# Loading the last three batches of a mixture of softmaxes head by head, instead of the last two

## Chip, cores and metric

One core of one Trainium2 chip. The metric is device time in microseconds (us), the median of several runs; less is better.

## The reference

32 batches, 128 positions, 4 heads, a vocabulary of 4096, all float32. Each head's logits go through a softmax over the vocabulary, and the four are added with weights that are a softmax of `prior`:

```python
# logits (32, 128, 4, 4096), prior (32, 128, 4)
prior_probs = softmax(prior, axis=-1)
softmax = np.exp(logits - logits.max(-1, keepdims=True)); softmax /= softmax.sum(-1, keepdims=True)
mixture = np.sum(prior_probs[..., None] * softmax, axis=2)      # (32, 128, 4096)
```

268 MB are read and 67 MB written: 8 MB (MiB) in and 2 MB out for each batch.

## The kernel before

Positions lie on the 128 partitions. Three engines matter: ACT (ScalarE) computes the exponentials, DVE (VectorE) scales and adds them, and SP (SyncE) issues the transfers to and from memory. A transfer is shared by 16 DMA engines, which move it in *packets*: here one packet is the contiguous bytes of one partition, 64 KB for four heads and 16 KB for one. A batch is one load tile of 4 heads x 16 KB per partition. Two such tiles are in use in turn, and so are two exponential tiles (`etile`) and two accumulators (`acc`). All loads of logits and all stores are issued by SP into one DMA queue, in program order.

```python
lpool = tile_pool(name="lpool", bufs=2)   # load tiles, 64 KB per partition each
epool = tile_pool(name="epool", bufs=2)   # exponentials of one head, 16 KB
apool = tile_pool(name="apool", bufs=2)   # accumulator of one batch, 16 KB

def pieces(b):
    return 1 if b >= B - 2 else H         # heads per transfer

def load(b):
    lt = lpool.tile([P, H, V], FP32, name="ltile")
    n = pieces(b)
    for h in range(0, H, n):
        nc.sync.dma_start(out=lt[:, h : h + n], in_=logits[b, :, h : h + n, :])
    ltiles[b] = lt

load(0); ...; load(1); ...                # and the softmax of prior: cut
for b in range(B):
    last, inplace = b == B - 1, b >= B - 2
    lt = ltiles.pop(b)
    acc = lt[:, 0] if inplace else apool.tile(...)
    for h in range(H):
        split = last and h == H - 1
        et = lt[:, h] if inplace else epool.tile(...)
        nc.scalar.activation(et, lt[:, h], AF.Exp, accum_out=dsum)         # L98, ACT
        # coeff = prior weight / dsum: two small DVE operations, L101 and L102
        if h == 0:   nc.vector.tensor_scalar_mul(acc, et, coeff)           # L104, DVE
        elif not split: nc.vector.scalar_tensor_tensor(acc, et, coeff, acc, mult, add)  # L106
        else:        ...  # the same in four chunks, two stores of 1 MB: L112
    if b + 2 < B: load(b + 2)             # issue L45; waits until ACT has read the whole tile of b
    if b < B - 4: store(b)                # issue L51
    elif b == B - 3: store(b - 1); store(b)
    elif b == B - 2: store(b)
```

So at the end the queue holds: load 28, store 26, load 29, store 27, load 30, load 31, store 28, store 29, store 30, and store 31 in two halves. Batches 30 and 31, which are loaded head by head, also work in place in their load tile.

The softmax here doesn't subtract the row's maximum and nothing guards it: scores larger than these inputs give would overflow.

## Time and profile before

| | before |
|---|---|
| time, median of 3 runs | 786.17 us (785.93 to 786.95) |
| steady batch (first exponential to first exponential) | 24.18 us, 10.49 MB |
| landing step of an 8 MB load, late in the run | 19.31 us |
| landing step of a 2 MB store | 4.87 us |
| loads 30 and 31, in four transfers each | 19.55 and 19.57 us |

A *landing* is the moment when the last of the 16 DMA engines has reported a transfer complete, as recorded in the trace. A *step* is the time from the landing before it in the queue to this one.

From the page of the kernel before: span; DVE and ACT busy time; GB/s in 40 equal slices; the queue with its share of the 16 engines' span; the chain that ended last; and two groups (busy us, mean ns of one | idle before them, and who ended it).

```profile
span 784.6 us, 1001 instructions
...
DVE 547.3 (70%) x408; ACT 472.6 (60%) x258; POOL 0.2 (0%) x4
...
GB/s 378 428 438 451 428 428 407 452 434 421 428 423 446 457 424 434 417 427 443 428 428 435 426 455 431 435 428 416 446 428 451 431 428 426 449 428 413 428 433 307
...
q1 hardware_dynamic: 10224, 335.55, 99.4%
...
DMA 63%; DVE 16%; ACT 13%; issue 6%; DVEq 0%; ACTq 0%; SPq 0%
...
L98 ACT ACTIVATE etile<-ltile 128x4096 f32<-128x4096 f32 x120 | 433.4, 3612 | 280.8 <-DMA ltile<-in_logits_dram 241.5
...
L104 DVE TENSOR_SCALAR acc<-etile,coeff 128x4096 f32<-128x4096 f32 x30 | 70.6, 2353 | 22.1 <-DMA out_dram<-acc 22.0
...
```

The compute engines are idle 30 and 40% of the time; the one DMA queue is busy for 99.4% of the span. Two stretches of the kernel before (columns: stretch, length, busy time and instructions of DVE, ACT, POOL, TensorE clock, DMA share, GB/s):

```profile
...
core 0: us, DVE busy (x) ACT busy (x) POOL busy (x), PEclk, DMA share, GB/s
300.00:690.00 390.00, 272.07 (x194) 235.59 (x128) 0.00 (x0) 1.00 1.00 433
765.00:785.00 20.00, 10.83 (x10) 2.44 (x2) 0.00 (x0) 1.00 0.72 303
...
```

433 GB/s in the middle lies at the ceiling: the Trainium skill, "DMA: Bandwidth & Descriptors", Specifications, gives 435 GB/s as the fabric limit of one core, and this trace agrees. The last 20 us are far below it (303 GB/s), as the 16 engines run out of work one after another.

The stretch that the change touches, from the timeline of the kernel before (start us, length us, engine, line, operation; in brackets how long the engine was idle before it and who ended that):

```profile
...
693.22 0.34 SPq L51 DMA_DIRECT2D out_dram<-acc  x1
...
711.64 25.92 SPq L45 DMA_DIRECT2D ltile<-in_logits_dram  x8
...
719.76 3.62 ACT L98 ACTIVATE etile<-ltile 128x4096 f32<-128x4096 f32 x1 [8.15 <-DMA ltile<-in_logits_dram]
...
724.63 2.35 DVE L104 TENSOR_SCALAR acc<-etile,coeff 128x4096 f32<-128x4096 f32 x1 [0.77 <-DMA out_dram<-acc]
...
727.08 3.62 ACT L98 ACTIVATE etile<-ltile 128x4096 f32<-128x4096 f32 x1
...
732.07 3.62 ACT L98 ACTIVATE etile<-ltile 128x4096 f32<-128x4096 f32 x1 [1.29 <-DVE rden L101]
...
```

Store 27 is issued at 693.22. At 711.64 begin the issues of loads 30 and 31 (eight, merged into one line). The exponentials of batch 29 start at 719.76, when load 29 has landed. DVE's first long step of batch 29 (the scaling, L104) starts at 724.63: its accumulator was free when store 27, which stands behind load 29 in the queue, had landed. The third and fourth exponentials follow at 727.08 and 732.07, each when DVE has given back an etile.

### The profile page before, as it was taken

What the parts mean: (1) busy time and instruction counts of PE and PEld (TensorE: products, weight loads), DVE (VectorE), ACT (ScalarE), POOL (GpSimd) and SP (SyncE); (2) the same over time, 40 slices, a digit from 0 to 9 for tenths busy, and PEclk for the clock granted to TensorE, in tenths of its full rate; (3) what the DMA queues carried; (4) which work ended last, traced back from release to release, by engine and by line L of the source; (5) the groups of instructions that cost most, each with busy time, mean ns of one, the idle gap of its engine ahead of it and who ended that gap; (6) DMA issues with size and microseconds to landing.
All of it is one profiled execution on the core that took longest, in us unless ns stands there. A gap on an engine that the chain in (4) does not pass through costs nothing.

```text
span 784.6 us, 1001 instructions
## 1 busy us (share of the span) xinstructions
DVE 547.3 (70%) x408; ACT 472.6 (60%) x258; POOL 0.2 (0%) x4
## 2 busy tenths in 40 slices
DVE  3588567866678666786667866668756687666995
ACT  0777554675546755467555676555765557755981
POOL 0000000000000000000000000000000000000000
DMA  9999999999999999999999999999999999999997
GB/s 378 428 438 451 428 428 407 452 434 421 428 423 446 457 424 434 417 427 443 428 428 435 426 455 431 435 428 416 446 428 451 431 428 426 449 428 413 428 433 307
DMA packets 10280, 335.68 MB, mean 428 GB/s; under 512 B 1152, under 2 KB 1152, under 8 KB 1184
## 3 DMA queue, kind: packets, MB, share of 16 engines
q1 hardware_dynamic: 10224, 335.55, 99.4%
q10 hardware_dynamic: 48, 0.07, 0.0%
q14 instruction: 8, 0.07, 0.0%
HBM read 268.50 MB, written 67.11 MB: 428 GB/s over the span
## 4 chain that ended last, share of the span: by engine, by line
DMA 63%; DVE 16%; ACT 13%; issue 6%; DVEq 0%; ACTq 0%; SPq 0%
DMA ltile<-in_logits_dram 59%; ACT etile L98 13%; DVE acc L106 11%; DMA out_dram<-acc 3%; DVE ltile L106 3%; DVE ltile L104 1%; DVE rden L101 1%; DVE coeff L102 1%; DVE ltile L112 0%; DVE acc L104 0%; DVEq L152 0%; ACTq L98 0%; SPq L45 0%; DVEq L104 0%
## 5 line engine op out<-in xcount | busy, mean ns | idle before, releaser
L98 ACT ACTIVATE etile<-ltile 128x4096 f32<-128x4096 f32 x120 | 433.4, 3612 | 280.8 <-DMA ltile<-in_logits_dram 241.5
L106 DVE SCALAR_TENSOR_TENSOR acc<-etile,coeff,acc 128x4096 f32<-128x4096 f32 x90 | 403.6, 4484 | 3.2
L101 DVE RECIPROCAL rden<-dsum 128x1 f32<-128x1 f32 x128 | 20.4, 160 | 186.4 <-ACT etile L98 183.3
L104 DVE TENSOR_SCALAR acc<-etile,coeff 128x4096 f32<-128x4096 f32 x30 | 70.6, 2353 | 22.1 <-DMA out_dram<-acc 22.0
L98 ACT ACTIVATE ltile<-ltile 128x4096 f32<-128x4096 f32 x8 | 28.8, 3606 | 2.5 <-DVE coeff L102 1.2
L102 DVE TENSOR_TENSOR coeff<-rden,pp 128x1 f32<-128x1 f32 x128 | 20.4, 159 | 4.4
L106 DVE SCALAR_TENSOR_TENSOR ltile<-ltile,coeff 128x4096 f32<-128x4096 f32 x5 | 22.4, 4485 | 0.2
L98 ACT ACTIVATION_READ_ACCUMULATOR etile<-ltile 128x1 f32 x120 | 22.4, 186 | 0.0
L60 DVE TENSOR_REDUCE pmax<-pr 32x128 f32<-32x512 f32 x1 | 0.7, 674 | 11.4 <-DMA pr<-in_prior_dram 11.4
L64 ACT ACTIVATE pe<-pc 32x512 f32<-32x512 f32 x1 | 0.6, 628 | 10.4 <-DVE pc L62 10.4
L112 DVE SCALAR_TENSOR_TENSOR ltile<-ltile,coeff 128x1024 f32<-128x1024 f32 x4 | 4.9, 1278 | 0.0
L104 DVE TENSOR_SCALAR ltile<-ltile,coeff 128x4096 f32<-128x4096 f32 x2 | 4.7, 2354 | 0.1
L64 ACT ACT_TABLE_LOAD x1 | 1.3, 1283 | 1.2 <-PEq L141 1.2
L78 DVE STREAM_TRANSPOSE pp<-pn 32x32 f32<-32x32 f32 x16 | 1.9, 170 | 0.1
L98 ACT ACTIVATION_READ_ACCUMULATOR ltile<-ltile 128x1 f32 x8 | 1.5, 186 | 0.0
L66 DVE TENSOR_REDUCE psum<-pe 32x128 f32<-32x512 f32 x1 | 0.7, 675 | 0.7 <-ACT pe L64 0.7
L71 DVE TENSOR_TENSOR pn<-pe,prec 32x512 f32<-32x512 f32 x1 | 1.0, 1020 | 0.0
L68 DVE RECIPROCAL prec<-psum 32x128 f32<-32x128 f32 x1 | 0.9, 942 | 0.0
L62 DVE TENSOR_TENSOR pc<-pr,pmax 32x512 f32<-32x512 f32 x1 | 0.7, 679 | 0.0
L141 POOL MEMSET const-bfloat16-1.0<- 128x1 bf16 x1 | 0.1, 101 | 0.0
L141 POOL MEMSET const-uint8-127<- 128x1 uint8 x1 | 0.1, 101 | 0.0
L141 POOL MEMSET const-float32-0.0<- 128x1 f32 x1 | 0.1, 98 | 0.2 <-issue 0.2
(1 smaller groups left out, 0.1 us busy)
## 6 DMA issues: line engine op xcount, KB each, us to landing
out_dram<-acc SPq DMA_DIRECT2D x30, 2048.0 KB, 31.4
ltile<-in_logits_dram SPq DMA_DIRECT2D x8, 2048.0 KB, 22.2
out_dram<-ltile SPq DMA_DIRECT2D x1, 2048.0 KB, 20.4
out_dram<-ltile SPq DMA_DIRECT2D x2, 1024.0 KB, 7.8
ltile<-in_logits_dram SPq DMA_DIRECT2D x30, 32.3
pr<-in_prior_dram ACTq DMA_DIRECT2D x1, 64.0 KB, 10.7
```

What stands on the lines that cost most here:

```text
L60: nc.vector.reduce_max(pmax, pr, axis=AX.X)
L62: nc.vector.tensor_sub(pc, pr, pmax.unsqueeze(2).to_broadcast([B, S, H]))
L64: nc.scalar.activation(pe, pc, AF.Exp)
L68: nc.vector.reciprocal(prec, psum)
L71: nc.vector.tensor_mul(pn.rearrange("b h s -> b s h"), pe, prec.unsqueeze(2).to_broadcast([B, S, H]))
L78: nc.vector.transpose(pp[32 * t : 32 * (t + 1), h, :], pn[:, h, 32 * t : 32 * (t + 1)])
L98: nc.scalar.activation(et, lt[:, h], AF.Exp, accum_out=dsum)
L101: nc.vector.reciprocal(rden, dsum)
L102: nc.vector.tensor_mul(coeff, rden, pp[:, h, b : b + 1])
L104: nc.vector.tensor_scalar_mul(out=acc, in0=et, scalar1=coeff)
L106: nc.vector.scalar_tensor_tensor(out=acc, in0=et, scalar=coeff, in1=acc, op0=ALU.mult, op1=ALU.add)
L112: nc.vector.scalar_tensor_tensor(out=acc[:, cs], in0=et[:, cs], scalar=coeff, in1=acc[:, cs], op0=ALU.mult, op1=ALU.add,)
```

## The change

Its intent is to let the third last batch, too, start on its first head instead of waiting for all four, to shorten the end of the kernel.

```diff
     def pieces(b):
-        return 1 if b >= B - 2 else H
+        return 1 if b >= B - 3 else H
```

Only batch 29 changes: four transfers of 2 MB with packets of 16 KB, where there was one of 8 MB with packets of 64 KB. Batch 29 keeps its separate accumulator and exponential tiles.

## The prediction

> **What bounds the kernel now.** The DMA queue, end to end. The page gives it 99.4% of the 16 engines' span (335.5 MB, 428 GB/s), against DVE 70% and ACT 60%. A steady batch takes 24.18 us (first exponentials at 647.22 and 671.40 in the timeline) and moves 10.49 MB: 434 GB/s. The Trainium skill, "DMA: Bandwidth & Descriptors", Specifications, has 435 GB/s as the fabric ceiling; the trace agrees. The trace's landings step 19.31 us for an 8 MB load and 4.87 us for a 2 MB store, without a gap, to the end: the last three stores land at 778.98, 781.41 and 783.84 of a span of 784.65.
>
> **What the change does.** Batch 29 is loaded by four 2 MB transfers (16 KB per partition) instead of one of 8 MB (64 KB). Bytes, order in the queue, exponentials and vector work stay. Three DMA issues (0.33 to 0.43 us) are added on an idle sequencer.
>
> *Intended gain:* batch 29's first exponential, which waits 8.2 us for the whole load (timeline, 719.76), may start at about 712.5, when batch 28 frees the buffers: 7 us earlier. It leads nowhere. The vector engine's first step of batch 29 waits for the accumulator, freed by the store of batch 27, which lands at 724.53, behind the whole load of 29. The third exponential waits for an etile buffer from that step, the fourth for the next. So the last exponential of batch 29 still ends at about 735.6, and the load of batch 31, which needs the whole buffer, is issued as late as now. Even if it went out earlier, the queue has 8 us of backlog there.
>
> *Cost:* a 16 KB packet takes 611 ns in the trace, a 64 KB packet 2418, and 4 x 611 = 2444. Loads 30 and 31, in pieces already, step 19.55 and 19.57 us per batch, against 19.31 to 19.33. My estimate is +0.24 us, all on the critical path, because the queue is. The fixed 2 us per DMA (same page, "Anatomy of one DMA") will not show: the pieces of loads 30 and 31 run back to back in this trace.
>
> **Time:** 786.17 + 0.24 = 786.4 us. Range 785.7 to 787.3, from the runs' spread (785.93 to 786.95) and chance: an instruction fetch on the same DMA engines (at 774.7) makes one landing step 5.63 instead of 4.87 us; the change could move such a hit by 0.8 us either way. Faster by over 2%: 0.5%; within 2%: 99%; slower by over 2%: 0.5%.
>
> **What would show each step.** Pieces of load 29 landing near 705.0, 709.9, 714.8 and 719.9. First exponential of batch 29 near 712.5; the ACT-on-load waits fall by about 8 us, from 241.5. The vector engine's wait for the store of batch 27 grows from 0.8 to about 7 us. Third and fourth exponentials of batch 29 at about 727.3 and 732.3, the issue of load 31 at about 735.9, and all later landings, 0.2 to 0.3 later than now. DMA share still 99%.
>
> **What would make it wrong.** If smaller transfers let the slowest of the 16 engines catch up (they land up to 4.9 us apart), the time could fall by tenths of a us or more. If the extra transfers use up completion semaphores and a later issue waits for an old one, a queue gap appears and the time rises by several us. If load 29 and store 27 changed places in the queue, the accumulator's wait would change too.

## The result, and the profile after

| | before | after |
|---|---|---|
| first comparison, median | 786.39 us (4 runs) | 785.82 us (785.24 to 786.54, 4 runs) |
| ratio, 95% interval | | 0.9993, 0.9976 to 1.001 |
| second comparison, median | 785.95 us (9 runs) | 786.36 us (785.70 to 786.97, 5 runs) |
| ratio, 95% interval | | 1.0007, 0.9995 to 1.002 |

Ratios and intervals are taken from the times of the fast runs and not from the medians, so a ratio is not quite that of the medians quoted beside it. The time is the same: once 0.6 us under, once 0.4 us over, while the kernel before alone scatters from 784.72 to 787.11.

The same lines of the page of the changed kernel:

```profile
span 783.5 us, 1004 instructions
...
DVE 547.2 (70%) x408; ACT 472.7 (60%) x258; POOL 0.2 (0%) x4
...
GB/s 385 458 405 415 428 435 417 460 432 435 428 407 449 428 428 432 441 426 458 432 428 421 428 443 428 432 442 417 464 432 432 428 412 445 432 421 432 431 428 343
...
q1 hardware_dynamic: 10656, 335.55, 99.6%
...
DMA 62%; DVE 18%; ACT 12%; issue 6%; DVEq 0%; ACTq 0%; SPq 0%
...
L98 ACT ACTIVATE etile<-ltile 128x4096 f32<-128x4096 f32 x120 | 433.5, 3613 | 279.4 <-DMA ltile<-in_logits_dram 232.4
...
L104 DVE TENSOR_SCALAR acc<-etile,coeff 128x4096 f32<-128x4096 f32 x30 | 70.6, 2353 | 24.9 <-DMA out_dram<-acc 24.9
...
```

And its stretches, with the columns as above:

```profile
...
core 0: us, DVE busy (x) ACT busy (x) POOL busy (x), PEclk, DMA share, GB/s
300.00:690.00 390.00, 273.57 (x196) 235.62 (x128) 0.00 (x0) 1.00 1.00 433
765.00:785.00 20.00, 9.31 (x7) 1.33 (x2) 0.00 (x0) 1.00 0.73 311
...
```

The timeline of the changed kernel at the same place:

```profile
...
691.92 0.34 SPq L51 DMA_DIRECT2D out_dram<-acc  x1
...
710.32 25.62 SPq L45 DMA_DIRECT2D ltile<-in_logits_dram  x8
...
711.37 3.62 ACT L98 ACTIVATE etile<-ltile 128x4096 f32<-128x4096 f32 x1 [1.07 <-issue]
...
719.90 0.16 DVE L101 RECIPROCAL rden<-dsum 128x1 f32<-128x1 f32 x1 [3.56 <-ACT etile L98]
...
723.49 2.35 DVE L104 TENSOR_SCALAR acc<-etile,coeff 128x4096 f32<-128x4096 f32 x1 [3.24 <-DMA out_dram<-acc]
...
725.93 3.62 ACT L98 ACTIVATE etile<-ltile 128x4096 f32<-128x4096 f32 x1 [6.07 <-issue]
...
730.45 3.62 ACT L98 ACTIVATE etile<-ltile 128x4096 f32<-128x4096 f32 x1 [0.81 <-ACT etile L98]
...
```

This profiled run is 1.32 us ahead of the profiled run of before when load 28 lands (694.17 against 695.49), a point up to which both kernels issue the same work. Take that off before comparing. Then:

- The first exponential of batch 29 starts at 711.37 instead of 719.76: the intended gain is there. ("issue" in its brackets means that the profile shows no releaser; it starts 0.1 us after a DVE step of batch 28 has ended and given back an etile. So does the one at 725.93, after DVE's multiplication.)
- It is spent on waiting. DVE idles 3.56 us ahead of the reciprocal at 719.90 and 3.24 us more for store 27, whose landing starts the multiplication at 723.49. The third and fourth exponentials, at 725.93 and 730.45, are as late as before (727.25 and 731.77 with the 1.32 us added).

The sums over the whole run, from the waits of before and then of after (engine and line, what it waited for: us in total, times, longest us):

```profile
...
ACT etile L98 <- DMA ltile<-in_logits_dram: 241.5, 30, 10.1
...
DVE acc L104 <- DMA out_dram<-acc: 22.0, 28, 1.2
...
```

```profile
...
ACT etile L98 <- DMA ltile<-in_logits_dram: 232.4, 29, 10.0
...
DVE acc L104 <- DMA out_dram<-acc: 24.9, 28, 3.2
...
```

ACT's wait for loads falls by 9.1 us, and the longest wait of DVE for a store grows from 1.2 to 3.2 us.

The landings show what the queue paid:

| landing, us | before | after | after, second profile |
|---|---|---|---|
| load 28 | 695.49 | 694.17 | 694.89 |
| store 27 (load 29 is ahead of it) | 724.53 | 723.47 | 724.16 |
| difference | 29.05 | 29.30 | 29.27 |
| last store | 783.84 | 782.48 | 783.47 |
| load 28 to last store | 88.35 | 88.31 | 88.57 |

(Differences are taken before rounding.) From the landing of load 28 to that of store 27, with store 26 and load 29 between them, it takes 0.25 and 0.22 us longer; load 29 alone steps 19.50 and 19.53 us, instead of 19.31. That the whole tail of the first profile is nevertheless not longer seems to have another reason: an instruction fetch on the DMA engines (at 774.7 us before, at 773.4 after) comes just ahead of a long landing step of store 30, 5.63 us in before, 5.34 us in after and 5.61 us in the second profile, instead of 4.87. Take off the excess of each and the tails are 87.59, 87.84 and 87.83 us: +0.25 and +0.24.

And the 1.32 us at the start? In the kernel before, a fetch at 558.7 us is followed by one load step of 20.19 instead of 19.31 us; in the changed kernel a fetch at 559.5 us is followed by a step of 19.30. In these profiles a fetch occupies one engine for 0.31 us, and the packet behind it takes 0.25 to 0.64 us longer than others of its size. At 558.7 us that is 0.31 + 0.60 us, near the 0.88 us by which the step is longer. In the landings it shows only in some of the profiles, as one would expect if it counts only where it meets the engine that is furthest behind (argued, not tested). The rest of the 1.32 us was there at load 16 (404.39 against 403.96), from uneven steps in the first 400 us. So the 1.2 us by which the profile's span is shorter (783.46 against 784.65) arose ahead of the changed load.

### The profile page after: what moved, and what is told of

Read it like the earlier page. It is cut to its first block, busy times and chain, and to the rows that moved or that the text cites. A ratio compares the mean times of both kernels' runs of the same rounds, so it can differ in the third digit from the quotient of the medians.

```text
span 783.5 us, 1004 instructions
## 1 busy us (share of the span) xinstructions
DVE 547.2 (70%) x408; ACT 472.7 (60%) x258; POOL 0.2 (0%) x4
## 4 chain that ended last, share of the span: by engine, by line
DMA 62%; DVE 18%; ACT 12%; issue 6%; DVEq 0%; ACTq 0%; SPq 0%
DMA ltile<-in_logits_dram 55%; ACT etile L98 12%; DVE acc L106 12%; DMA out_dram<-acc 8%; DVE ltile L106 3%; DVE coeff L102 1%; DVE acc L104 1%; DVE ltile L104 1%; DVE rden L101 1%; DVE ltile L112 0%; DVEq L152 0%; ACTq L98 0%; SPq L45 0%; DVEq L104 0%
```

## The experiments

Theory: the queue is the bound from end to end; an early start of batch 29 buys nothing, and pieces cost 0.24 us per batch. Rivals: pieces are free or help (the first comparison had that sign); the early start would pay if the accumulator did not block it; and, on where the 0.24 us come from, the packet size or the number of transfers. The first four ran on one chip, with five rounds and a median of 785.81 us for before (11 runs); the other four likewise, with 785.95 us (9 runs).

### 1. All batches in pieces

```diff
-        return 1 if b >= B - 2 else H
+        return 1
```

> All 32 batches are loaded head by head, so the 30 batches that the kernel before loads whole are changed at once. My theory (the queue is the bound, and an 8 MB load costs 0.24 us more in pieces): 30 x 0.24 = +7.2 us, about 793.6 us, ratio 1.009 to before; steady load steps in the landings 19.55 instead of 19.31 us; no queue gap. Rival A (the 0.24 us is no real cost, the changed kernel was 0.6 us faster, so pieces are free or help): ratio 0.997 to 1.001. Rival B (more waits for completion semaphores appear): several per cent slower with the DMA share below 98%.

Measured: 790.94 us, +5.1, ratio 1.0067 (1.0054 to 1.008). From its page (packets and queue), and then a stretch of it with the columns as above:

```profile
...
DMA packets 23240, 335.69 MB, mean 425 GB/s; under 512 B 2592, under 2 KB 2592, under 8 KB 2624
...
q1 hardware_dynamic: 23184, 335.55, 99.8%
...
```

```profile
...
300.00:690.00 390.00, 266.96 (x193) 235.90 (x127) 0.00 (x0) 1.00 1.01 430
...
```

No gap appears in the queue (99.8%), but over the same stretch it moves 430 instead of 433 GB/s. So pieces do cost time, and Rivals A and B fall. The size is less than the 7.2 us I had summed. A late load step is 19.53 us, not the 19.55 that I took from loads 30 and 31 of before. From load 16 to load 28 a batch takes 24.48 us (before: 24.26), +0.22, near the 0.24 of the sum (each of the two stretches holds one long step, 20.19 us in before and a store step of 5.87 us here); from load 2 to load 16 it takes 24.49 (before: 24.43), only +0.06. In that early part the kernel before loses time as well, to 64 KB packets that take 0.1 to 0.7 us more than their usual 2.42 us, mostly just ahead of a load's landing. 14 batches x 0.16 us would be 2.2 us, about what is missing. But these steps are from one profile each, and the early part differs between profiles of the same code too: the six profiles of kernels that do the same work up to load 28 (before, after and runs 4 to 7) show 24.29 to 24.43 us per batch early and 24.18 to 24.26 us late. So a late cost of 0.2 to 0.3 us is firm, the early 0.06 is not, and where the missing 2.1 us went is not shown. Why those packets stall was not settled.

### 2. One transfer, but 16 KB packets

```diff
-        lt = lpool.tile([P, H, V], FP32, name="ltile")
+        lt = lpool.tile([P, H, V + 16], FP32, name="ltile")[:, :, 0:V]
```

> The kernel before, its load tile padded by 64 bytes per partition behind each head, so that a whole 8 MB load is still one transfer but of 16 KB packets. If the cost of pieces comes from the packet size (a 64 KB packet takes 2418 ns, four of 16 KB 2444): 30 x 8 x 26 ns = +6.2 us, ratio 1.008. If it comes from the number of transfers: +0, ratio 1.000.

Measured: 789.66 us, +3.9, ratio 1.0049 (1.0037 to 1.0061). The late load step is 19.46 us, against 19.31 with 64 KB packets and 19.53 with four transfers (run 1). The same stretch of it:

```profile
...
300.00:690.00 390.00, 269.96 (x193) 234.87 (x128) 0.00 (x0) 1.00 1.01 431
...
```

Both seem to be part of it: of the 0.22 us, 0.15 come with the smaller packets and 0.07 with the three additional transfers, from one profile each. (The padding also moves where each head lies in its partition; no run separates that from the packet size.) My 6.2 us was too much: the sum of packet durations (4 x 611 against 2418 ns) overstates what the queue loses.

### 3. Four transfers, but 64 KB packets (failed)

```diff
+        if n == H:
+            for p in range(0, P, 32):
+                nc.sync.dma_start(out=lt[p : p + 32], in_=logits[b, p : p + 32])
```

> The kernel before, its 30 whole loads cut into four transfers of 32 partitions each, so four transfers as in pieces, but with packets of 64 KB. If the cost comes from the packet size: three more completion packets of 9 ns per load, 30 x 0.03 = +0.8 us, ratio 1.001. If it comes from the number of transfers: +7.2 us, ratio 1.009.

Measured: 1415.21 us (six runs, 1383.57 to 1423.38). Its runs scatter so much that the profiled one counts as slow (over 1.5% above the fastest of this kernel), so no ratio is given; the size leaves no doubt. From its page:

```profile
...
DMA packets 11721, 335.69 MB, mean 236 GB/s; under 512 B 2592, under 2 KB 2592, under 8 KB 2624
...
q1 hardware_dynamic: 11664, 335.55, 99.1%
...
```

A 64 KB packet took 5085 ns instead of 2418. Neither theory had that in it. The Trainium skill, "SBUF — State Buffer", section "Door 1: The DMA port swizzle", says that 32 adjacent partitions reach only 8 of the 16 ports of the memory, for about 218 GB/s, and this run agrees: a quarter load of 2.10 MB lands every 10.1 us or so, which makes 208 GB/s. I had not looked there. (That the ports are the cause is the page's reason; no run here varies them alone.) The experiment changed the ports together with the number of transfers, so it says nothing about its own question; experiments 2 and 8 answer that.

### 4. Store 27 ahead of load 29

In the changed kernel, to take away what blocks batch 29:

```diff
+        if b == B - 5:
+            store(b)
         if b + 2 < B:
             load(b + 2)
-        if b < B - 4:
+        if b < B - 5:
             store(b)
```

> The changed kernel, with the store of batch 27 put ahead of the load of batch 29 in the queue, so that the vector engine's first step of batch 29 finds its accumulator free. My theory: the wait for the store of batch 27 goes from 3.2 us to 0, the exponentials of batch 29 end about 7 us earlier (about 728.8 instead of 735.6 in before's time), the load of batch 31 is issued as much earlier, and the time does not move, because the queue had backlog there: ratio to before 0.999 to 1.001. Rival (the early start of batch 29 is worth something once the accumulator no longer blocks it): 2 us or more faster, ratio 0.997 or lower.

Measured: 786.22 us, +0.4, ratio 1.0007 (0.9995 to 1.002). Its timeline at the same place, and its wait for stores:

```profile
...
692.25 0.34 SPq L51 DMA_DIRECT2D out_dram<-acc  x1
692.70 37.96 SPq L45 DMA_DIRECT2D ltile<-in_logits_dram  x12
...
716.69 2.35 DVE L104 TENSOR_SCALAR acc<-etile,coeff 128x4096 f32<-128x4096 f32 x1
...
720.08 3.60 ACT L98 ACTIVATE etile<-ltile 128x4096 f32<-128x4096 f32 x1
...
725.17 3.62 ACT L98 ACTIVATE etile<-ltile 128x4096 f32<-128x4096 f32 x1 [1.40 <-DVE rden L101]
...
```

```profile
...
DVE acc L104 <- DMA out_dram<-acc: 21.3, 27, 1.1
...
```

The block is gone: the first long DVE step of batch 29 starts at 716.69, the fourth exponential ends at 728.79, and load 31 is issued at 728.91 instead of 735.81 (before). This profile is 1.0 us ahead of before at load 28, so that is 5.9 us earlier, where I had expected about 7. And the time does not move; the last store lands at 782.79, 88.30 us after load 28, with 0.43 us of excess at store 29 from a fetch: 87.87 us without it, as in the changed kernel. The last piece of load 30 had still to land, at 743.34, so the earlier issue only waited longer in the queue. This separates the two reasons of the prediction: the accumulator's wait did hold batch 29, but it cost nothing.

### 5. The change once more

The changed kernel, unedited.

> The changed kernel once more, with more rounds, because its first four runs had a median 0.6 us under that of before and my sum says 0.24 us over it. My theory: the two differ by less than the runs of one kernel scatter (before: 784.72 to 787.11 us), ratio 0.999 to 1.001, and the step from the landing of load 28 to that of store 27 is 29.3 us in the profile, against 29.04 in before. Rival (the change really gains): ratio 0.9993 again with an interval that leaves out 1.

Measured: 786.36 us, ratio 1.0007 (0.9995 to 1.002), and 29.27 us from load 28 to store 27. The sign of the first comparison was within the noise. A loss of 0.24 us (0.03%) fits, but no interval here is narrow enough to show it in the time; it is shown in the landings only.

### 6. No batch in pieces

```diff
-        return 1 if b >= B - 2 else H
+        return H
```

> No batch is loaded head by head. If pieces pay only where the queue runs dry: batch 31 lands whole at about 763.2 us in before's time, its vector chain then ends near 785.5 us instead of 776.0, the queue is empty between store 30 and the two last stores, and the time is about 6 us longer, 792 us, ratio 1.008. If pieces never paid here: ratio 0.999.

Measured: 791.72 us, +5.8, ratio 1.0075 (1.0061 to 1.0089). Two lines of its timeline, and the busy tenths of the 16 DMA engines in 40 slices of 765 to 790 us (0.625 us each), first of before and then of this run:

```profile
...
762.85 3.62 ACT L98 ACTIVATE ltile<-ltile 128x4096 f32<-128x4096 f32 x1 [4.90 <-DMA ltile<-in_logits_dram]
...
780.16 4.87 DVE L112 SCALAR_TENSOR_TENSOR ltile<-ltile,coeff 128x1024 f32<-128x1024 f32 x4
```

```profile
...
DMA  9999999999995449999999933211000000000000
...
```

```profile
...
DMA  9999999999994332210000000000059999999500
...
```

Load 31 lands whole at 762.77, all of its work comes after that, and the last DVE steps start at 780.16 (771.10 before). In the middle of its tenths stands a row of zeros: the queue is empty until the last two stores are issued at 782.67 and 785.06. Here a wait for data reaches the end.

### 7. Only the last batch in pieces

```diff
-        return 1 if b >= B - 2 else H
+        return 1 if b >= B - 1 else H
```

> Only batch 31 is loaded head by head. Batch 30 then lands whole at about 743.8 us, its exponentials start there instead of at 735.7, the vector chain of 30 and 31 ends near 783.6 us instead of 776.0, past the 3.4 us of slack that it has in before, and the time is about 4.3 us longer, 790.5 us, ratio 1.005. Rival (only the last batch matters): ratio 1.000.

Measured: 789.68 us, +3.7, ratio 1.0047 (1.0034 to 1.006). The same stretch of DMA:

```profile
...
DMA  9999999999994433200000000059999999500000
...
```

The gap is shorter (the last two stores are issued at 780.72 and 783.12), but it is there. The step from 1 to 2 batches in pieces closes it; with 2 the last two stores are issued at 773.61 and 776.00, before the queue is empty, and land in sequence. Not every engine is still at work then: the first of the 16 has finished store 30 at 773.27 (the dip to 4 in the tenths of before), the last only at 778.98, and it is the last that the end waits for. The step from 2 to 3 has nothing left to close. Run 4 bears that out: counted from the landing of load 28 it issues the last two stores 3.0 us earlier than before, and ends no sooner.

### 8. Two transfers of two heads

```diff
-        return 1 if b >= B - 2 else H
+        return 1 if b >= B - 2 else 2
```

> The kernel before, with its 30 whole loads in two transfers of two heads each (packets of 32 KB). A cost per packet and a cost per transfer, fitted to the late load steps of the runs with one transfer of 16 KB packets (19.45 instead of 19.31 us) and with four (19.55 us): 8 more packets per engine give +0.047 us, one more transfer +0.033 us, so a late load step of 19.39 us and at most 30 x 0.08 = +2.4 us, ratio 1.001 to 1.003. A cost that came from the number of transfers alone would give 19.39 too, one from the packets alone 19.36.

Measured: 787.68 us, +1.7, ratio 1.0023 (1.0011 to 1.0036); late loads step 9.69 us per half, 19.38 per load. The same stretch of it:

```profile
...
300.00:690.00 390.00, 269.29 (x193) 237.41 (x129) 0.00 (x0) 1.00 1.00 432
...
```

The sum of a cost per packet and a cost per transfer meets the step (19.39 expected), but 0.03 us between its variants is too fine to tell them apart here. The order of the late steps, 19.31, 19.38, 19.46 and 19.53 us, with 433, 432, 431 and 430 GB/s, is the result.

No version beats the kernel before. With 2 batches in pieces the engine that is furthest behind has no gap, and the bytes alone need 335.5 / 0.435 = 771 us (an estimate from the 435 GB/s of the Trainium skill, "DMA: Bandwidth & Descriptors", Specifications); where the remaining 13 us or so of the span go was not broken down.

## Why the prediction was right

- **The bound.** Right. Taking away a wait (4) moved nothing; making packets smaller (1, 2, 8) moved the time although the compute work stayed.
- **The gain leads nowhere.** Right, with its mechanism: the first exponential at 711.37 (about 712.5 predicted; 712.69 with the profile's 1.32 us added), then a wait for store 27. The predicted single wait of "about 7 us" shows as two, 3.56 + 3.24 = 6.8 us, because in the built program the reciprocal and coefficient of head 1 stand ahead of the scaling of head 0 (719.90 and 723.49 in the timeline above).
- **The issue of load 31 "0.2 to 0.3 later".** Wrong in sign. It was at 734.19, or 735.51 with the 1.32 us added, against 735.81: 0.3 us earlier. I had copied the order of DVE's instructions from before. With head 1's coefficient ready, the step at 725.88 followed the scaling directly, which gave the etile back 0.5 us sooner. It cost or gained nothing, as there was backlog.
- **"My estimate is +0.24 us, all on the critical path".** Right in the landings (+0.25 and +0.22, the tail +0.25 and +0.24), and not resolved in the time: medians -0.6 and +0.4 us in two comparisons. A forecast of no change at all would have fitted the times as well; what carries the sum are the landings and run 1. Its first support, the packet durations, was weaker than I took it for: they would give 0.21 us for packets alone, and one transfer with such packets cost 0.15 (2). The observed steps of loads 30 and 31 were the sound evidence, since they contain both costs, if a little high (19.55 and 19.57, where run 1 has 19.53).
- **The fixed 2 us per DMA "will not show".** Right: the trace shows the pieces of load 29 stepping 4.83 to 4.91 us, like those of loads 30 and 31. The cited section gives the 2 us for transfers that GpSimd issues, and these are issued by SP; the conclusion rests on the trace alone.
- **Chance of 0.8 us from a fetch.** Right in kind and size: 0.76, 0.47 and 0.74 us of excess at store 30 in three profiles, and 0.9 and 1.0 us after the fetch at 558 us in two of them.
- **"If smaller transfers let the slowest of the 16 engines catch up".** They did not: with all batches in pieces (1) the first and the last engine were 4.37 us apart at load 28, against 4.90 in before and 3.28 and 4.43 in the two profiles of the changed kernel, whose work up to there is that of before.

## What to carry to other kernels

Cutting a load so that work can start sooner pays only where the DMA queue would otherwise run dry; count the batches at the end for which it does (two here), and stop there, since each further cut costs a little of a full queue's rate. When an engine waits for data that arrives at the full rate of the queue, shortening the wait gains nothing: look instead at whether the last transfers are issued before the queue is empty. And when the expected effect is smaller than the scatter of the runs, enlarge it (all batches instead of one) rather than repeat it.

## What the Trainium skill lacked or had wrong

- "DMA: Bandwidth & Descriptors", section "Anatomy of one DMA": it gives about 2 us of fixed cost per DMA (for the GpSimd path), and lacks what of it is left in a queue that is full. Here three more transfers cost about 0.07 us together, and smaller packets (16 instead of 64 KB) about 0.15 us per 8 MB.
- The same page, section "Where 436 GB/s comes from": "For HBM↔SBUF transfers the HBM side (~358) binds". The sentence lacks its condition. This core, with loads and stores between HBM and SBUF, moved 433 GB/s for 390 us. (The page has 425 and 408.7 GB/s for one core alone in other sections, and ties about 358 to both cores of a pair streaming.)
- "Runtime: NRT & Kernel Launch", section "Instruction fetch mechanics": the cost of crossing a 16 KiB boundary is called "mostly hidden", and what a fetch costs a full DMA queue is lacking. Here a fetch (one packet of 8 KB) ran on the engines that move the data: it took 0.31 us, the packet behind it took 0.25 to 0.64 us longer, and in some profiles a landing step that was 0.9 us longer followed (20.19 instead of 19.31).
- No page has how far the 16 engines drift apart in one long queue: the first and last of them to finish a transfer were 0.2 to 0.7 us apart at the first 8 MB load and 3.3 to 5.3 us apart at load 28 in every run but the one with partitions split. The lead grew at the uneven steps of the first 400 us and at fetches (in before from 3.99 to 4.88 us at load 23), stayed as it was over the even steps between them, and was not won back. The kernel ends with the last engine.
